# Attention logits of two units at a time, shorter projection stretches, and a written-out order of steps

## The chip, the cores and the metric

The kernel runs on one core of a Trainium2 chip. The metric is the device time of one execution in microseconds (us); smaller is better. Five engines work side by side, each through its own instructions in order: PE (the matrix engine; the trace keeps its weight loads apart as PEld), DVE (vector), ACT (activation), POOL and SP. SP here only starts DMAs. They wait for one another through semaphores.

## The reference

A trunk of two decoder layers over 512 tokens of width 1024, in float32. The first layer (a Mamba-2 mixer and a convolutional feed-forward net) and both feed-forward nets are not touched by this change. The part in question is the differential attention of the second layer, with 8 heads, two softmax maps per head (c = 0, 1) and 64 numbers per map, over keys and values that were projected once:

```python
logits = jnp.einsum('bqhcd,bkhcd->bhcqk', qblk, k).astype(jnp.float32) * scale
logits = logits + bias[None, :, None]
logits = jnp.where(dist >= 0, logits, -jnp.inf)
p = jax.nn.softmax(logits, axis=-1)
attn = p[:, :, 0] - lam * p[:, :, 1]
return jnp.einsum('bhqk,bkhd->bqhd', attn.astype(v.dtype), v)
...
o = rms_norm(o, subln_g) * (1.0 - lam_init)
return o.reshape(b, s, V_TOTAL) @ out_w
```

## The kernel before

Every large product is done as three matmuls of 128x128 weights by 512 columns (high part times high part, high by low, low by high). In the attention stage these large products are the projections: values of heads 0 to 3 (`v0`), queries of heads 4 to 7 (`q1`), values of heads 4 to 7 (`v1`), and the output projection of heads 0 to 3 (`attn_out(0, ...)`). They are chained into one generator, `fill`, and the attention proper is put between pieces of it. A call of `next(fill)` issues the next stretch. In `proj` (L1326) a stretch is two token blocks, which is 12 matmuls; in `attn_out` it is 6.

The attention is cut into units. A head has three: query blocks 0 and 1 together, block 2, and block 3 (`PARTS`), with 384, 384 and 512 columns of keys up to the diagonal. A unit goes through these steps:

- `logits()`: the matmuls at L1514, queries times keys, one bank of PSUM for each of the two maps. The two maps use the two halves of PE's rows and run side by side. Then DVE adds the bias and finds the maximum, from PSUM into SBUF (L1520), and ACT takes the exponential and its sum (L1527).
- `weigh()`: a reciprocal and a small product on DVE (L1532, L1533), then p0 + factor * p1 (L1537).
- `turn()`: 3 or 4 transposes on PE (L1546) into one bank, copied to SBUF by ACT (L1547).
- `values()`: transposed weights times values on PE (L1557) into one bank, copied by ACT (L1560).

When the three units of a head are through, `normed_out` normalises the head on DVE and ACT (L1567 to L1573), and `turned_out` transposes it on PE (L1579), with two copies out (L1583 on ACT, L1584 on DVE).

All these small banks, those of the transposes of keys and queries (L1373, copied by ACT at L1375) too, come from one ring of four auxiliary banks:

```python
def aux_bank(name):
    return pp.tile([P, T], F32, tag="aux", name=name)
```

The fifth request waits until the first bank has been read. The large products have four banks of their own (`mm_bank`). The copies of the values projection out of those banks are at L1480, on ACT; weights are split into high and low parts by ACT (L173, L148) and DVE (L174, L159).

The order on PE in this stage is the order in which the code is written (`manual_schedule` for PE alone); for DVE and ACT a scheduler orders the work, so the lists on those two engines move with the code too. Before the change the order came from a list of "places", from which the code worked out, by counters, which unit is turned, weighed and valued when. Apart from the first place, which does two units' logits together, each place did: transposes of one unit, logits of one unit, weighted values of an earlier unit, then one or two stretches. In the names of the trace, `lg` is logits, `at` transposed weights, `po` weighted values, `oT` the turned head, `ps_v`, `ps_q` and `ps_ao` the banks of the projections; `lg4_2` in an instruction list is head 4, part 2.

Of the kernel before, what the change touches and what calls it, by code (L numbers as in the profile page):

```python
# [42 lines left out]
def trunk_kernel(ctx: ExitStack, tc, x, ssm_ln_g, ssm_in_w, ssm_conv_w, ssm_conv_b, ssm_dt_bias,  # L43
# [60 lines left out]
    def tok_order(key):  # L104
        return (2, 6, 0, 4) if key == "q0" else range(0, KB, 2)
# [1187 lines left out]
    with tc.tile_pool(name="att", bufs=1) as ap, ExitStack() as later:  # L1293
# [32 lines left out]
        def proj(key, evac):  # L1326
            pss = [mm_bank("ps_%s_%d" % (key, b)) for b in range(NT)]
            order = tok_order(key)
            for k0 in order:
                wh, wl = chunk("%s_%d" % (key, k0))  # L1330
                for b in range(NT):
                    ts = slice(b * P, (b + 1) * P)
                    for k in range(k0, k0 + 2):
                        st, sp_ = k == order[0], k == order[-1] + 1
                        pe.matmul(pss[b], xgh[k][:, ts], wh[:, k - k0, :], start=st, stop=False)
                        pe.matmul(pss[b], xgh[k][:, ts], wl[:, k - k0, :], start=False, stop=False)
                        pe.matmul(pss[b], xgl[k][:, ts], wh[:, k - k0, :], start=False, stop=sp_)
# [12 lines left out]

        def squared(key, t, rt, out, b):
            s = ap.tile([P, T], F32, tag="ksq", name="ksq%s_%d" % (key, b), bufs=1)
# [128 lines left out]
            yield from proj(key, evac)  # L1481

        PARTS = ((0, 1), (2,), (3,))
        fl = lambda a: a.rearrange("p a b -> p (a b)")

        class Unit:


            def __init__(self, h, part, st):
                self.h, self.part, self.st = h, part, st  # L1490
                self.tag = "%d_%d" % (h, part)
                self.ii = PARTS[part]
                self.off = (0, P)
# [55 lines left out]
            def values(self):  # L1549
                h = self.h  # L1550
                if self.part == 0:
                    self.st["ot"] = up.tile([P, NT, P], F32, tag="ot", name="ot%d" % h, bufs=2)
                ps = aux_bank("po" + self.tag)
                for j, i in enumerate(self.ii):
                    o = self.off[j]
                    for k in range(i + 1):
                        pe.matmul(ps[:, j * P:(j + 1) * P], self.at[:, o + k * P:o + (k + 1) * P],  # L1557
                                  vt[k][:, h * P:(h + 1) * P], start=(k == 0), stop=(k == i))
                k = len(self.ii)
                act.activation(self.st["ot"][:, self.ii[0]:self.ii[0] + k, :],  # L1560
                               ps[:, :k * P].rearrange("p (a d) -> p a d", a=k), AF.Copy)

        def normed_out(h, st):
            ot = st["ot"]
            sq = ap.tile([P, T], F32, tag="ksq", name="osq%d" % h, bufs=1)
            so = up.tile([P, NT], F32, tag="so", name="so%d" % h, bufs=2)
            act.activation(sq, fl(ot), AF.Square)  # L1567
            dve.reduce_sum(so, sq.rearrange("p (a q) -> p a q", a=NT), axis=AX.X)
            e = up.tile([P, NT], F32, tag="eps", name="eps%d" % h, bufs=2)
            s0 = st["sm"][:, :, 0]  # L1570
            dve.scalar_tensor_tensor(out=e, in0=s0, scalar=EPS, in1=s0, op0=ALU.mult, op1=ALU.mult)
            rsqrt_act(so, ap, "o%d" % h, [P, NT], P, e)
            dve.tensor_tensor(out=ot, in0=ot, in1=so.unsqueeze(2).to_broadcast([P, NT, P]), op=ALU.mult)  # L1573
# [14 lines left out]
        os = []  # L1588
# [45 lines left out]
        with tc.manual_schedule(engines={mybir.EngineType.PE}):  # L1634
            run(qk("q0", qT[0], 49, (("2", 1), ("5", 0))))
            with tc.tile_pool(name="keys", bufs=1) as kc:
                keys(kc)
            op_ = later.enter_context(tc.tile_pool(name="att_o", bufs=1))
            up = later.enter_context(tc.tile_pool(name="units", bufs=1))
            fill = chain(vproj("v0", 0), qk("q1", qT[1], 49, ((2, 0), (2, 1))), vproj("v1", 1),  # L1640
                         attn_out(0, None, range(KB)))
            us = []
            for h in range(AH):
                st = {}
                us += [Unit(h, part, st) for part in range(len(PARTS))]
            n = len(us)

            ots, valued_heads = [], []
            for _ in range(5):
                next(fill)  # L1650

            def values(t):
                u = us[t]
                u.values()
                if u.part == len(PARTS) - 1:
                    valued_heads.append(u)
                    ots.append([t + 5, u])
# [6 lines left out]
            def out_of(t):  # L1664
                if ots and ots[0][0] <= t:
                    u = ots.pop(0)[1]
                    os.append(turned_out(u.h, u.st))

            turned = valued = weighed = t = 0

            def turn_to(m):
                nonlocal turned
                while turned < min(m, n):
                    us[turned].turn()
                    turned += 1

            def weigh_to(m):
                nonlocal weighed
                while weighed < min(m, n):
                    us[weighed].weigh()  # L1680
                    weighed += 1

            def values_to(m):
                nonlocal valued
                while valued < min(m, n):
                    values(valued)
                    valued += 1

            for places in [(2, 2), 1, 1, 1, 1, 1, 1, 1, 1, 2, 1, 1, 1, 1, 1, 2, 1, 2, 1, 2, 1, 2, 2, 1, 1, 1]:
                if isinstance(places, tuple):  # L1690
                    weigh_to(t)
                    turn_to(t - 1)
                    values_to(t - 2)
                    norm_heads()
                    turn_to(t)
                    next(fill)
                    out_of(t + 1)
                    values_to(t)
                    norm_heads()
                    next(fill)  # L1700
                    us[t].logits()
                    us[t + 1].logits()
                    weigh_to(t + 1)
                    next(fill)
                    weigh_to(t + 2)
                    next(fill)
                    t += 2
                    continue
                turn_to(t - 1)
                if t == n - 5:  # L1710
                    weigh_to(t)
                    with tc.issue_after(us[t - 1].weighed):
                        us[t].logits()
                elif t < n:
                    us[t].logits()
                weigh_to(t)
                values_to(t - 2)
                for i in range(places):
                    if places == 1 and t < 16:
                        out_of(t)  # L1720
                    next(fill)
                    if i == 0 and (places > 1 or t > n):
                        out_of(t)
                    if valued_heads and os:
# [3 lines left out]
                t += 1  # L1728
            assert next(fill, None) is None
            last_out(norm1)  # L1730

# [37 lines left out]
```

## Time and profile before

| | |
|---|---|
| median of 3 timed runs | 1318.3 us (1318.17 to 1318.86) |
| the profiled execution | 1318.13 us, of which the span from first to last instruction is 1316.3 us |
| DVE busy over the span | 1069.5 us (81%) |
| ACT busy over the span | 713.6 us (54%) |
| first and last logit matmul of the stage | 811.5 us and 928.8 us from the span's start |
| granted PE clock in this stage | 1.00 |

A matmul that is recorded as busy may overlap the next one, because PE is a pipeline. So the time that a group of matmuls costs is read from one start to the next start, not from the busy column. A matmul with float32 operands (logits and weighted values) appears as two records, two passes with one weight load each; the transposes and the large products appear as one.

### The profile page before, as it was taken

To read this page: it belongs to the slowest core of one execution; us is meant where nothing else is said; L and a number is where in the kernel's file an instruction comes from. 1 tells how busy PE (TensorE), PEld (TensorE's weight loads), DVE (VectorE), ACT (ScalarE), POOL (GpSimd) and SP (SyncE) were. 2 spreads that over 40 slices of the span, in tenths; PEclk is the share of its full clock that TensorE was granted. 3 is DMA by queue.
4 is the path that set the end of the run, shared out by engine and by line. 5 is a ranking of instruction groups with operands and counts; after the bars stand their busy time and mean duration, and the time that the engine had idled before them with its cause. 6 is when DMAs were issued, how large, how long until landed. Compare 5 with 4: busy or idle time off the path is not lost.

```text
span 1316.3 us, 18256 instructions
## 1 busy us (share of the span) xinstructions
PE 1311.2 (100%) x6771; PEld 1096.9 (83%) x6771; DVE 1069.5 (81%) x1774; ACT 713.6 (54%) x1156; POOL 178.1 (14%) x244
## 2 busy tenths in 40 slices
PE   9999999999999999999999999999999999999998
PEld 8878888888888988898889887777788888888887
DVE  7989878888878877876888877677778878887886
ACT  6696554743354445544556667767654544544452
POOL 5230200300021401120113210000020100010001
PEclk9999999999999999999999999999999999999999
DMA  7553433432235657673866754211224445453625
GB/s 209 156 153 90 149 101 108 140 95 85 84 96 138 126 139 204 179 161 113 220 164 145 197 124 128 69 60 64 65 80 160 98 119 183 105 96 112 192 64 128
DMA packets 202552, 167.84 MB, mean 128 GB/s; under 512 B 7580, under 2 KB 175904, under 8 KB 202464
## 3 DMA queue, kind: packets, MB, share of 16 engines
q1 hardware_dynamic: 176080, 124.93, 31.7%
q0 software_dynamic: 22928, 36.46, 14.7%
q10 hardware_dynamic: 3456, 5.30, 1.1%
q8 instruction: 53, 0.87, 0.3%
q14 instruction: 35, 0.29, 0.1%
HBM read 160.21 MB, written 6.44 MB: 127 GB/s over the span
## 4 chain that ended last, share of the span: by engine, by line
PE 98%; ACT 1%; DVE 1%; issue 0%; DVEq 0%
PE ps_g L209 6%; PE ps_u L209 6%; PE ps_g L208 6%; PE ps_u L208 6%; PE ps_u L210 6%; PE ps_g L210 6%; PE ps_in L208 5%; PE ps_in L210 5%; PE ps_in L209 5%; PE ps_s L1239 3%; PE ps_s L1244 3%; PE ps_s L1242 3%; PE ps_s L1144 3%; PE ps_s L1146 3%; PE ps_s L1141 3%; PE ps_o L209 2%
## 5 line engine op out<-in xcount | busy, mean ns | idle before, releaser
L208 PE MATMUL ps_u<-xgh,wh_u 128*128 128x512 f32 x352 | 137.4, 390 | 0.0
L209 PE MATMUL ps_g<-xgl,wh_g 128*128 128x512 f32 x352 | 137.1, 390 | 0.0
L208 PE MATMUL ps_g<-xgh,wh_g 128*128 128x512 f32 x352 | 137.1, 389 | 0.0
L210 PE MATMUL ps_u<-xgh,wl_u 128*128 128x512 f32 x352 | 137.0, 389 | 0.0
L209 PE MATMUL ps_u<-xgl,wh_u 128*128 128x512 f32 x352 | 137.0, 389 | 0.0
L210 PE MATMUL ps_g<-xgh,wl_g 128*128 128x512 f32 x352 | 137.0, 389 | 0.0
L208 PE MATMUL ps_in<-xgh,wh_in 128*128 128x512 f32 x304 | 123.0, 404 | 0.0
L210 PE MATMUL ps_in<-xgh,wl_in 128*128 128x512 f32 x304 | 119.7, 394 | 0.0
L209 PE MATMUL ps_in<-xgl,wh_in 128*128 128x512 f32 x304 | 119.2, 392 | 0.0
L209 PEld LDWEIGHTS ps_g<-xgl,wh_g 128*128 128x128 f32 x352 | 66.1, 188 | 13.8 <-DVE xgl L488 0.3
L210 PEld LDWEIGHTS ps_u<-xgh,wl_u 128*128 128x128 f32 x352 | 66.1, 188 | 13.7
L1244 PE MATMUL ps_s<-sl,wh_s 128*128 128x256 f32 x308 | 77.5, 283 | 0.0
L208 PEld LDWEIGHTS ps_g<-xgh,wh_g 128*128 128x128 f32 x352 | 66.1, 188 | 13.7
L1242 PE MATMUL ps_s<-sh,wh_s 128*128 128x256 f32 x308 | 77.5, 283 | 0.0
L210 PEld LDWEIGHTS ps_g<-xgh,wl_g 128*128 128x128 f32 x352 | 66.1, 188 | 13.6
L208 PEld LDWEIGHTS ps_u<-xgh,wh_u 128*128 128x128 f32 x352 | 66.1, 188 | 13.6
L209 PEld LDWEIGHTS ps_u<-xgl,wh_u 128*128 128x128 f32 x352 | 66.1, 188 | 13.5
L1126 ACT ACTIVATE sh<-vg 128x256 fp32r<-128x256 f32 (+1 forms) x44 | 23.1, 524 | 98.5 <-DVE vg L1276 98.4
L1052 POOL DMA_DIRECT2D wz<-in_ffn_down_w_dram x36 | 44.2, 1296 | 235.8 <-DVE wl_s L1080 167.9
L1024 DVE SCALAR_TENSOR_TENSOR vg<-ug,cf,vg 128x511 f32<-128x511 f32 x88 | 65.8, 747 | 5.5 <-ACT vg L1022 4.1
L1272 ACT ACTIVATE vg<-vg 128x512 f32<-128x512 f32 x44 | 27.8, 633 | 78.2 <-DVE vg L1024 78.1
L1021 DVE TENSOR_TENSOR uu<-ps_u,nr_f 128x512 f32<-128x512 f32 x44 | 30.3, 689 | 46.7 <-PE ps_u L210 46.7
(425 smaller groups left out, 3501.2 us busy)
## 6 DMA issues: line engine op xcount, KB each, us to landing
wr_g<-in_ffn_up_w_dram SPq DMA_DIRECT2D x44, 512.0 KB, 3.9
wr_u<-in_ffn_up_w_dram SPq DMA_DIRECT2D x44, 512.0 KB, 3.9
wr_in<-in_ssm_in_w_dram SPq DMA_DIRECT2D x40, 512.0 KB, 3.8
wz<-in_ffn_down_w_dram POOLq DMA_DIRECT2D x27, 512.0 KB, 5.8
m<-cumd POOLq DMA_DIRECT2D x16, 512.0 KB, 4.7
wr_out<-in_ssm_out_w_dram SPq DMA_DIRECT2D x16, 512.0 KB, 3.4
wr_s<-in_ffn_down_w_dram SPq DMA_DIRECT2D x13, 512.0 KB, 3.7
xT<-in_ffn_down_w_dram SPq DMA_DIRECT2D x10, 512.0 KB, 6.8
```

What stands on the lines that cost most here:

```text
L208: pe.matmul(ps, wh, xh, start=start, stop=False)
L209: pe.matmul(ps, wh, xl, start=False, stop=False)
L210: return pe.matmul(ps, wl, xh, start=False, stop=stop).ins
L1021: dve.tensor_tensor(out=u, in0=ps, in1=r, op=ALU.mult)
L1024: dve.scalar_tensor_tensor(out=v[:, s:], in0=u[:, :T - s], scalar=col(2 - s), in1=v[:, s:], op0=ALU.mult, op1=ALU.add)
L1052: pool.dma_start(view(t, nq), source(p0, c, nq, j, i), accum_op=ALU.add)
L1141: pe.matmul(pss[b], h, ws[q][1][:, cols], start=False, stop=end and q == qs[-1], skip_group_check=more)
L1144: pe.matmul(pss[b], h, ws[q][0][:, cols], start=first and q == qs[0], stop=False, skip_group_check=more)
L1146: pe.matmul(pss[b], w, ws[q][0][:, cols], start=False, stop=False, skip_group_check=more)
L1239: pe.matmul(v[:, b], wl[:, q, cols], h, start=False, stop=q == nq - 1, skip_group_check=not opens or b > 0)
L1242: pe.matmul(v[:, b], wh[:, q, cols], h, start=opens and q + b == 0, stop=False, skip_group_check=not opens or b > 0)
L1244: pe.matmul(v[:, b], wh[:, q, cols], w, start=False, stop=False, skip_group_check=not opens or b > 0)
```

## The change

Three edits. First, `proj` gives way after every token block and not after every second one, so that a stretch of a projection is 6 matmuls. Secondly, the logits of two units are issued together over four auxiliary banks (a step written `L`), followed by the weighing of both. Thirdly, the counters are gone: a string of letters says where each stretch (`f`), each unit's transposes (`a`), each unit's weighted values (`v`) and each turned head (`o`) stands. The amount of computation stays the same: 24 units, 24 turns, 24 values, 64 stretches of 6 matmuls (where it was 24 of 12 and 16 of 6).

```diff
@@ proj
                             for i in (b - 1, b):
                                 evac(i, pss[i], rts[0])
-                        yield
+                    yield
@@
         PARTS = ((0, 1), (2,), (3,))
+        ORDER = ("f f L f f a f",
+                 "L f a f v f v f a f",
+                 "L f a f v f v f a f",
+                 "L f a f v f v f o a f",
+                 "L f a f v f v f o a f",
+                 "L f a f v f v f a f",
+                 "L f a f v f v o a f",
+                 "L f a f v f f v o a f",
+                 "L f a v f v a f",
+                 "L f a v f v o a f",
+                 "L f a v f v o a f",
+                 "L f a v f v a f",
+                 "f a v f o v f")
@@
-            for _ in range(5):
+            for _ in range(10):
                 next(fill)
...
-            for places in [(2, 2), 1, 1, 1, 1, 1, 1, 1, 1, 2, 1, 1, 1, 1, 1, 2, 1, 2, 1, 2, 1, 2, 2, 1, 1, 1]:
...
-                turn_to(t - 1)
-                if t == n - 5:
-                    weigh_to(t)
-                    with tc.issue_after(us[t - 1].weighed):
-                        us[t].logits()
-                elif t < n:
-                    us[t].logits()
-                weigh_to(t)
-                values_to(t - 2)
-                for i in range(places):
-                    if places == 1 and t < 16:
-                        out_of(t)
-                    next(fill)
-                    if i == 0 and (places > 1 or t > n):
-                        out_of(t)
...
+            steps = {"f": lambda: next(fill), "a": lambda: next(turned).turn(), "v": values, "o": head_out}
+            pairs = iter(zip(us[::2], us[1::2]))
+            for step in " ".join(ORDER).split():
+                if step == "L":
+                    pair = next(pairs)
+                    for u in pair:
+                        u.logits()
+                    for u in pair:
+                        u.weigh()
+                else:
+                    steps[step]()
             assert next(fill, None) is None
             last_out(norm1)
```

Two places show what this does to the engines' lists. Lines from L1497 on are 13 higher after the change (L1514 is L1527, L1546 is L1559, and so on).

**The first logits.** On PE, at the boundary between the third and the last weight chunk of `v0`, before (-) and after (+):

```order
 L1336 MATMUL ps_v0_3_7495<-wl_v0_4_7499,xgh_86 128x512
 L1337 MATMUL ps_v0_3_7495<-wh_v0_4_7498,xgl_87 128x512
+L1527 MATMUL lg0_0_0_7622<-kT0_6903,qT0_6905 128x128
+L1527 MATMUL lg0_0_1_7623<-kT0_6903,qT0_6905 128x128
+L1527 MATMUL lg0_0_0_7622<-kT0_6903,qT0_6905 128x256
+L1527 MATMUL lg0_0_1_7623<-kT0_6903,qT0_6905 128x256
+L1527 MATMUL lg0_1_0_7639<-kT0_6903,qT0_6905 128x384
+L1527 MATMUL lg0_1_1_7640<-kT0_6903,qT0_6905 128x384
 L1335 MATMUL ps_v0_0_7492<-wh_v0_6_7530,xgh_86 128x512
 L1336 MATMUL ps_v0_0_7492<-wl_v0_6_7531,xgh_86 128x512
```

The logits of the first two units stand 12 large matmuls earlier than before. On PE, 12 large matmuls further on, where the logits stood:

```order
 L1337 MATMUL ps_v0_1_7493<-wh_v0_6_7530,xgl_87 128x512
-L1514 MATMUL lg0_0_0_7644<-kT0_6903,qT0_6905 128x128
-L1514 MATMUL lg0_0_1_7645<-kT0_6903,qT0_6905 128x128
-L1514 MATMUL lg0_0_0_7644<-kT0_6903,qT0_6905 128x256
-L1514 MATMUL lg0_0_1_7645<-kT0_6903,qT0_6905 128x256
-L1514 MATMUL lg0_1_0_7661<-kT0_6903,qT0_6905 128x384
-L1514 MATMUL lg0_1_1_7662<-kT0_6903,qT0_6905 128x384
+L1559 MATMUL at0_0_7677<-ident_77,lg0_0_0_7620 128x128 x3
 L1335 MATMUL ps_v0_2_7494<-wh_v0_6_7530,xgh_86 128x512
```

Now the first unit's transposes stand there, two stretches behind its logits. On DVE, after the change, between the first reads of these logits and the weighing of the first unit:

```order
L1533 ISA lg0_1_1_7638,mx0_1_7636<-lg0_1_1_7640,tb0_7616 128x384
L1533 ISA mx0_1_7636 128x1
L1545 RECIPROCAL sm0_7618<-sm0_7618 128x2
L174 SCALAR_TENSOR_TENSOR wl_q1_2_7657<-wr_q1_2_7654,c2_89,wh_q1_2_7656 128x512
L1546 SCALAR_TENSOR_TENSOR sm0_7618<-sm0_7618,nlam_94 128x2
L1550 SCALAR_TENSOR_TENSOR lg0_0_0_7620<-lg0_0_1_7621,sm0_7618,lg0_0_0_7620 128x128
L1550 SCALAR_TENSOR_TENSOR lg0_0_0_7620<-lg0_0_1_7621,sm0_7618,lg0_0_0_7620 128x256
```

Before, both halves of the weight split `wl_q1_2` stood ahead of the reads; now one half stands ahead of them and the other inside the weighing.

**The first values of head 4.** They (`po4_0`) are the first to need the second half of the values, which ACT copies from the banks of `v1` into `vt0` to `vt3`. On ACT, before:

```order
L1547 ACTIVATE at4_0_8416<-at4_0_8417 128x384
L1527 ACTIVATE lg4_2_0_8423,sm4_8323<-lg4_2_0_8423,mx4_2_8422 128x512
L1527 ACTIVATE lg4_2_1_8424,sm4_8323<-lg4_2_1_8424,mx4_2_8422 128x512
L1560 ACTIVATE ot3_8344<-po3_2_8436 128x128
L1480 ACTIVATE vt0_6907<-ps_v1_0_8142,tr_nkv_6982 128x512
L1567 ACTIVATE osq3_8462<-ot3_8344 128x512
L1480 ACTIVATE vt1_6908<-ps_v1_1_8143,tr_nkv_6982 128x512
L1547 ACTIVATE at4_1_8477<-at4_1_8478 128x384
```

And on ACT after the change:

```order
L1540 ACTIVATE lg4_2_1_8448,sm4_8332<-lg4_2_1_8448,mx4_2_8446 128x512
L1540 ACTIVATE lg5_0_0_8461,sm5_8459<-lg5_0_0_8461,mx5_0_8460 128x128
L1480 ACTIVATE vt0_6907<-ps_v1_0_8146,tr_nkv_6982 128x512
L1540 ACTIVATE lg5_0_1_8462,sm5_8459<-lg5_0_1_8462,mx5_0_8460 128x128
L1540 ACTIVATE lg5_0_0_8461,sm5_8459<-lg5_0_0_8461,mx5_0_8460 128x256
L1540 ACTIVATE lg5_0_1_8462,sm5_8459<-lg5_0_1_8462,mx5_0_8460 128x256
L1560 ACTIVATE at4_1_8496<-at4_1_8497 128x384
L1480 ACTIVATE vt1_6908<-ps_v1_1_8147,tr_nkv_6982 128x512
L1573 ACTIVATE ot4_8510<-po4_0_8511 128x256
```

The copy `vt1`, without which `po4_0` cannot end, has moved from ahead of the exponentials of `lg5_0` to behind them. On DVE after the change, the reads of the same pair of units, whose results those exponentials need (rows of `mx` alone are the second half of the read above them):

```order
L1533 ISA lg4_2_0_8447,mx4_2_8446<-lg4_2_0_8449,tb4_8330 128x512
L1533 ISA mx4_2_8446 128x1
L501 TENSOR_TENSOR rst_o3_8417<-so3_8411 128x4
L159 TENSOR_TENSOR wl_ao0_1_8487<-wr_ao0_1_8484,wh_ao0_1_8486 128x1024
L502 SCALAR_TENSOR_TENSOR rst_o3_8417<-rst_o3_8417,rsm_o3_8416 128x4
L1533 ISA lg4_2_1_8448,mx4_2_8446<-lg4_2_1_8450,tb4_8330 128x512
L1533 ISA mx4_2_8446 128x1
L503 SCALAR_TENSOR_TENSOR so3_8411<-rst_o3_8417,so3_8411 128x4
L1533 ISA lg5_0_0_8461,mx5_0_8460<-lg5_0_0_8463,tb5_8457 128x128
L1533 ISA mx5_0_8460 128x1
L1586 TENSOR_TENSOR ot3_8306<-ot3_8306,so3_8411 128x512
L1533 ISA lg5_0_1_8462,mx5_0_8460<-lg5_0_1_8464,tb5_8457 128x128
```

Before, the two reads of `lg4_2` stood next to each other; now a weight split (`wl_ao0_1`) stands between them, and a product over a whole head (`ot3`) between the reads of `lg5_0`.

More of the change, by code (lines that the diff above doesn't have):

```diff
@@ L1645, in trunk_kernel @@
                 us += [Unit(h, part, st) for part in range(len(PARTS))]
-            n = len(us)
-            ots, valued_heads = [], []
-            for _ in range(5):
+            for _ in range(10):
                 next(fill)
[L1652 to L1657, printed above, removed]
+            turned, valued = iter(us), iter(us)
+            valued_heads, normed_heads = [], []
             def norm_heads():
@@ L1662, in norm_heads @@
                     normed_out(u.h, u.st)
[L1664 to L1687, printed above, removed]
-            for places in [(2, 2), 1, 1, 1, 1, 1, 1, 1, 1, 2, 1, 1, 1, 1, 1, 2, 1, 2, 1, 2, 1, 2, 2, 1, 1, 1]:
-                if isinstance(places, tuple):
-                    weigh_to(t)
-                    turn_to(t - 1)
-                    values_to(t - 2)
-                    norm_heads()
-                    turn_to(t)
-                    next(fill)
[L1697 to L1700, printed above, removed]
-                    us[t].logits()
[L1702 to L1709, printed above, removed]
-                if t == n - 5:
-                    weigh_to(t)
-                    with tc.issue_after(us[t - 1].weighed):
-                        us[t].logits()
-                elif t < n:
-                    us[t].logits()
-                weigh_to(t)
-                values_to(t - 2)
-                for i in range(places):
-                    if places == 1 and t < 16:
-                        out_of(t)
-                    next(fill)
-                    if i == 0 and (places > 1 or t > n):
-                        out_of(t)
-                    if valued_heads and os:
@@ L1725, in trunk_kernel, with values @@
+                    normed_heads.append(u)
+            def values():
+                u = next(valued)
+                u.values()
+                if u.part == len(PARTS) - 1:
+                    valued_heads.append(u)
+                    if os:
                         with tc.issue_after(state["ol"]):
```

4 lines of the change are left out of this document (3 added, 1 removed).

## The prediction

> **What bounds the kernel now.** I read the page first, then the attention stage alone.
>
> ```profile
> span 1316.3 us, 18256 instructions
> PE 1311.2 (100%) x6771; PEld 1096.9 (83%) x6771; DVE 1069.5 (81%) x1774; ACT 713.6 (54%) x1156; POOL 178.1 (14%) x244
> PE 98%; ACT 1%; DVE 1%; issue 0%; DVEq 0%
> 811.00:942.00 131.00, 130.92 (x737) 99.66 (x736) 96.66 (x307) 93.71 (x250) 0.00 (x0) 1.00 0.21 65
> ```
>
> The chain that ended last is PE for 98% of the span. The last row is the attention stage: of 131.00 us PE is busy 130.92, while DVE and ACT work for 96.66 and 93.71. So PE waits for nobody here, although DVE and ACT are some 70% full. The change can then do two things only: alter what PE's own sequence costs, or make PE wait. Both are read from starts in the timeline.
>
> **What PE's own sequence costs.** The first rows are the one place where two units' logits already stand together; the others show a unit alone, and transposes followed by values with no logits between.
>
> ```profile
> 811.00 0.39 PE L1336 MATMUL ps_v<-wl_v,xgh 128*128 128x512 f32 x1
> 811.23 0.39 PE L1337 MATMUL ps_v<-wh_v,xgl 128*128 128x512 f32 x1
> 811.55 1.57 PE L1514 MATMUL lg<-kT,qT 64*128 64x128 f32 x12
> 813.05 0.50 PE L1335 MATMUL ps_v<-wh_v,xgh 128*128 128x512 f32 x1
> 813.39 0.40 PE L1336 MATMUL ps_v<-wl_v,xgh 128*128 128x512 f32 x1
> ...
> 840.49 0.93 PE L1514 MATMUL lg<-kT,qT 64*128 64x128 f32 x8
> 841.34 0.94 PE L1557 MATMUL po<-vt,at 128*128 128x128 f32 x6
> 842.03 0.48 PE L1335 MATMUL ps_q<-wh_q,xgh 128*128 128x512 f32 x1
> 842.35 0.40 PE L1336 MATMUL ps_q<-wl_q,xgh 128*128 128x512 f32 x1
> 844.86 0.60 PE L1546 MATMUL at<-ident,lg 128*128 128x128 f32 x4
> 845.39 0.92 PE L1514 MATMUL lg<-kT,qT 64*128 64x384 f32 x4
> 846.24 0.94 PE L1557 MATMUL po<-vt,at 128*128 128x128 f32 x6
> ...
> 935.24 0.40 PE L210 MATMUL ps_ao<-oh,wl_ao 128*128 128x512 f32 x1
> 935.48 0.60 PE L1546 MATMUL at<-ident,lg 128*128 128x128 f32 x4
> 935.91 0.83 PE L1557 MATMUL po<-vt,at 128*128 128x128 f32 x6
> 936.50 0.48 PE L208 MATMUL ps_ao<-oh,wh_ao 128*128 128x512 f32 x1
> ```
>
> A large matmul follows the last in 0.23 us (811.00 to 811.23). Four transposes take 0.43 when values come next (935.48 to 935.91), 0.53 when logits come next (844.86 to 845.39): entering the half-row logits costs 0.10. Six records of values take 0.59 after transposes (935.91 to 936.50) and 0.69 after logits (841.34 to 842.03): leaving costs 0.10 in the next group. The two kinds of unit take 0.85 alone (840.49 to 841.34, 845.39 to 846.24), together 1.70, but the pair takes 1.50. Entered from and left for large matmuls, the pair pays the same single tolls (0.32 for 0.23, and 0.34 where 842.03 to 842.35 has 0.32). So a pair saves 0.20 + 0.10 + 0.10 = **0.40 us**. There are 12 pairs afterwards and one before: 11 x 0.40 = **4.4 us saved**. The bounds are 3.9 (the row of 0.34 taken as a full extra toll on that side) and 4.7.
>
> The shorter stretches cut the row of large matmuls oftener. A cut costs nothing I can see: 0.24 from a large matmul to transposes (935.24 to 935.48), and after values 0.32 that makes up for a last record of values shortened by about as much. Some 30 more cuts at 0.00 to 0.01 are under 0.3 us. The multiplications are as many as before. The bias loads of the next head are wanted one unit earlier:
>
> ```profile
> L1500 SPq DMA_DIRECT2D tb<-bd x8: 338/338/425, 792.9 to 903.9; - x8
> DMA to landing us min/median/max: 3.0/3.6/5.2
> ```
>
> They land 3.6 us after issue, and each has two buffers. A unit is 5 us of PE and the second buffer was last read a whole head ago, so I put the SP queue at nothing; if a load came behind a weight load on SP that waits, one L would start up to 3.6 us late.
>
> **Where PE will wait.** Until now, a unit's transposes came two units (10 us) behind its logits. In the new list they come two stretches behind at the start, four or five later, and ACT and DVE must read, exponentiate and weigh two units in that time. I added up the chains in the order that the changed lists have, with these durations.
>
> ```profile
> 812.51 0.29 DVE L1520 CUSTOM_DVE_ANT_0 lg<-lg,tb 128x128 f32<-128x128 f32 x1 [1.40 <-PE lg L1514]
> 812.72 0.42 DVE L1520 CUSTOM_DVE_ANT_0 lg<-lg,tb 128x256 f32<-128x256 f32 x1
> 815.20 0.75 DVE L1537 SCALAR_TENSOR_TENSOR lg<-lg,sm,lg 128x128 f32<-128x128 f32 x2
> 809.70 1.41 DVE L174 SCALAR_TENSOR_TENSOR wl_q<-wr_q,c,wh_q 128x512 fp32r<-128x512 f32 x2 [1.50 <-ACT wh_q L173]
> 850.64 1.13 PE L1514 MATMUL lg<-kT,qT 64*128 64x512 f32 x4
> 851.80 0.69 DVE L1520 CUSTOM_DVE_ANT_0 lg<-lg,tb 128x512 f32<-128x512 f32 x1 [0.70 <-PE lg L1514]
> L159 DVE TENSOR_TENSOR wl_ao<-wr_ao,wh_ao 128x1024 fp32r<-128x1024 f32 x7 | 8.6, 1222 | 2.4 <-ACT wh_ao L148 2.4
> L1573 DVE TENSOR_TENSOR ot<-ot,so 128x512 f32<-128x512 f32 x7 | 4.8, 687 | 0.1
> L1527 ACT ACTIVATE lg<-lg,mx 128x512 f32<-128x512 f32 x16 | 11.5, 717 | 8.5 <-DVE mx L1520 8.5
> L1527 ACT ACTIVATE lg<-lg,mx 128x256 f32<-128x256 f32 x16 | 8.0, 498 | 0.5 <-DVE mx L1520 0.5
> L1527 ACT ACTIVATE lg<-lg,mx 128x128 f32<-128x128 f32 x16 | 6.3, 392 | 2.4 <-DVE mx L1520 2.4
> L1547 ACT ACTIVATE at<-at 128x384 f32<-128x384 f32 x16 | 7.7, 481 | 2.6 <-PE at L1546 2.6
> L1480 ACT ACTIVATE vt<-ps_v,tr_nkv 128x512 f32<-128x512 f32 x7 | 4.6, 675 | 0.7 <-PE ps_v L1337 0.7
> ```
>
> Neighbours overlap: on DVE the next starts 0.08 before the row's end (812.51, 812.72), on ACT about 0.11; an exponential also reads its sum out, so that its step is about its mean.
>
> *First transposes.* Logits move from 811.55 to 808.83 (12 large matmuls). Before, logits to weighed took 815.20 + 0.75 - 811.55 = 4.40 us. Now one half of the weight split (809.70, 0.66) delays the first read from 809.79 to 810.36, and the other half, 0.66, stands inside the weighing, of which the quicker order of exponentials takes back 0.2: weighed at 808.83 + 4.40 + 0.57 + 0.46 = 814.26. PE is there after the pair, 1.50, a toll of 0.11 and two stretches, 12 x 0.23: 813.20. PE waits **1.1 to 1.2**.
>
> *Values of head 4.* Count from the first logit of the pair `lg4_2`, `lg5_0`. PE needs 1.8 (0.4 of pass time more than the pair of 1.50, with its exit), 1.38 for a stretch, 0.33 for three transposes, 1.38 again, and 0.45 for the blocks that need only `vt0`: it wants `vt1` at 5.3. DVE reads `lg4_2_0` at 1.16 (850.64 to 851.80), for 0.61; `wl_ao0_1` takes 1.14 and two tiny steps 0.16; so `lg4_2_1` is read from 3.07 to 3.76. ACT then does its exponential (to 4.5), one of 128 columns (4.9), the copy `vt0` (5.5), exponentials of 0.39, 0.49, 0.49 (6.8), the copy of the transposes, 0.37, and `vt1`, 0.68: 7.9. PE waits **2.6**. Behind it in PE's queue stand the rest of `v1` and all that follows.
>
> *Three in the output projection.* A pair holds all four auxiliary banks, so that the next transposes need DVE's first reads of it. Before `lg6_0`, DVE has two additions and a split `wl_ao0_3`; by the same sums `at5_2` waits 0.6. Its copy on ACT lies behind six exponentials, and `po5_2` waits 0.5; at the next pair `po6_1` waits 0.7 likewise. Ahead of that, `lg1_2` finds its bank still holding turned keys, 0.4.
>
> Together 1.2 + 2.6 + 0.6 + 0.5 + 0.7 + 0.4 = 6.0. A group that starts after a wait also has no weights loaded ahead; by the toll of 0.10 that is about 0.5 for these. Of the present list some 0.2 us of small waits go. So **6.3 us of waits**, with bounds 4.9 (no reload toll, ACT copies 0.2 sooner at each place) and 7.5 (two more places like `at5_2`).
>
> **The sum.** 6.3 - 4.4 = +1.9 us on the profiled execution, 1318.13 to 1320.0; the median of the runs lies 0.17 above that execution, so **1320.2 us**. The bounds give 4.9 - 4.7 = +0.2 to 7.5 - 3.9 = +3.6.
>
> [...]
>
> **Rivals.**
>
> *The waits are smaller than the saving.* The lists of DVE and ACT are fixed, but I took ACT's start behind each wait as late as the sums allow. If ACT and DVE, 70% full, run ahead at head 4, `vt1` is there in time and 2.6 goes; if the bank waits go too, only the start (1.2) and the keys (0.4) stay: 1.6 - 4.4 = -2.8, or 1315.5. Against it stands `wl_ao0_1`, which no order of arrival moves from between the two reads. It decides when `vt1` is copied before 5.3 on that scale.
>
> *The copy of transposed weights always comes last.* Slower: in each of the 11 pairs ACT runs the exponentials of both units ahead of a copy that PE waits for. Six exponentials are 3.0 us, one stretch is 1.38. If PE loses 0.7 in each, beside 1.2, 2.6 and 0.4, that is 7.7 + 4.2 - 4.4 = +7.5, 1325.8; half the pairs give about +3.7, 1322. It decides where a `v` stands one stretch behind an `a` that follows L. For it: in the last four pairs the list has just that. Against it: in the earlier pairs another stretch lies between, and the wait comes out at nothing there.
>
> *The clock falls.* The granted clock is 1.00 in the whole stage. In the kernel's first microseconds 13 records of a 128x128 matmul take 3.14 us, against 0.11 each for values:
>
> ```profile
> 1.14 3.14 PE L292 MATMUL warm<-ones 128*128 128x128 f32 x13 [1.14 <-DVE ones L219]
> ```
>
> So a cold start costs 3.14 - 13 x 0.11 = 1.7 us. If the wait at head 4 cooled PE, the time would be 1321.9. [...]
>
> **How the numbers follow.** The forecast gets 0.60, the smaller waits 0.17, the copies that come last 0.20, the clock 0.03. About 0.2% (2.6 us) is what a measurement here can tell from no change: 1315.7 to 1320.9. Of the forecast's own range, 1318.5 to 1321.9, I put 0.14 above that, of the slower rival 0.13, with the clock 0.30 in all; of the quicker rival 0.15 lies below. The rest, 0.55, is no change that can be told. The range of 8 in 10 goes to the quicker rival's 1315.5 and into the slower one, to 1323.0.
>
> **What would show it.** PE idle, now 0.1 us in the stage, should be about 6 in the profile after, with one wait of over 2 us for `vt` (L1480), one over 1 us for weighed logits at the first transposes, and half-microsecond ones at transposes and values behind the last pairs. A logit pair should take 1.5 to 1.7 us from start to start. Without the wait for `vt` the first rival is right; with waits in every pair the second; with pairs that take as long as two units apart, my saving is wrong.

## The result, and the profile after

| | median | range | runs |
|---|---|---|---|
| before | 1318.18 us | 1317.26 to 1319.03 | 22 |
| changed | 1320.03 us | 1319.09 to 1322.27 | 22 |

The changed kernel takes 1.0016 times the time of the one before (95% interval 1.0009 to 1.0022): 1.85 us more, where 1.9 were forecast. One of the 11 runs of experiment 1 below took 1444.79 us at a mean granted clock of 0.85, and is left out of its ratio. The page of the changed kernel's profile, busy times by engine and then the chain that ended last:

```profile
span 1317.4 us, 18264 instructions
PE 1308.4 (99%) x6771; PEld 1095.3 (83%) x6771; DVE 1071.5 (81%) x1774; ACT 713.3 (54%) x1156; POOL 178.3 (14%) x244
PE 96%; ACT 1%; DVE 1%; DMA 0%; issue 0%; SPq 0%; DVEq 0%; ACTq 0%
```

The attention stage by itself (stretch, its length, then busy time of PE, weight loads, DVE, ACT, POOL, and the granted clock):

```profile
811.00:942.00 131.00, 127.12 (x725) 98.43 (x725) 95.28 (x296) 92.01 (x246) 0.00 (x0) 1.00 0.21 65
```

PE idles 3.88 us of 131.00, where it idled 0.08. What it waited for, from 808 to 943 us (engine, line, what was waited for: us in total, times, longest):

```profile
PE po L1570 <- ACT vt L1480: 2.1, 2, 1.6
PE po L1570 <- ACT at L1560: 0.8, 2, 0.5
PE at L1559 <- DVE lg L1550: 0.6, 1, 0.6
PE at L1559 <- DVE mx L1533: 0.3, 1, 0.3
```

These are four of the five kinds of wait that the prediction named; the one for the bank of turned keys doesn't show as idle time. The prediction's sign of about 6 us of idle time did not come, and its wait of over 2 us for `vt` came as two, of 0.5 and 1.6. The view counts only what lies between the modelled end of one matmul and the start of the next (a large matmul is recorded for 0.39 us where the next starts after 0.23, so some 0.16 of a wait is hidden); the full loss is read from start to start. First how long the stage is: its first large matmul (`ps_v`) and its last (`ps_ao`), each with durations and the first and last start, before:

```profile
L1335 PE MATMUL ps_v<-wh_v,xgh x64: 389/389/504, 790.6 to 894.9; 128*128 128x512 f32 x64
...
L210 PE MATMUL ps_ao<-oh,wl_ao x64: 387/392/400, 898.2 to 963.0; 128*128 128x512 f32 x64
```

and after:

```profile
L1335 PE MATMUL ps_v<-wh_v,xgh x64: 389/397/504, 789.8 to 895.6; 128*128 128x512 f32 x64
...
L210 PE MATMUL ps_ao<-oh,wl_ao x64: 388/389/402, 898.3 to 963.9; 128*128 128x512 f32 x64
```

963.0 - 790.6 = 172.4 before, 963.9 - 789.8 = 174.1 after: the stage is 1.7 us longer. This execution also came 0.8 us earlier to the stage. That is no part of the change: in the 12 traces of this document the stage begins anywhere from 789.6 to 791.0. So its own time, 1319.09, lies only 0.96 above the 1318.13 of the profile before. In medians of 22 runs such differences count for less.

**First transposes.** PE and DVE after the change, in order of time (start, duration):

```profile
811.80 0.17 DVE L1545 RECIPROCAL sm<-sm 128x2 f32<-128x2 f32 x1
811.88 0.73 DVE L174 SCALAR_TENSOR_TENSOR wl_q<-wr_q,c,wh_q 128x512 fp32r<-128x512 f32 x1
812.21 0.39 PE L1337 MATMUL ps_v<-wh_v,xgl 128*128 128x512 f32 x1
812.53 0.21 DVE L1546 SCALAR_TENSOR_TENSOR sm<-sm,nlam 128x2 f32<-128x2 f32 x1
812.78 0.75 DVE L1550 SCALAR_TENSOR_TENSOR lg<-lg,sm,lg 128x128 f32<-128x128 f32 x2
813.19 0.83 PE L1559 MATMUL at<-ident,lg 128*128 128x128 f32 x3 [0.59 <-DVE lg L1550]
813.78 0.47 PE L1335 MATMUL ps_v<-wh_v,xgh 128*128 128x512 f32 x1
```

From the large matmul to the transposes it takes 0.98 us instead of 0.24, and the three transposes take 0.59 instead of 0.25, since the later ones wait for the second weighing: 1.08 lost. The weight split `wl_q` stands inside the weighing for 0.65, from 811.88 to 812.53.

**Values of head 4**, with DVE's and ACT's rows that count:

```profile
887.14 1.22 DVE L159 TENSOR_TENSOR wl_ao<-wr_ao,wh_ao 128x1024 fp32r<-128x1024 f32 x1
888.35 0.69 DVE L1533 CUSTOM_DVE_ANT_0 lg<-lg,tb 128x512 f32<-128x512 f32 x1
890.02 0.40 PE L1337 MATMUL ps_v<-wh_v,xgl 128*128 128x512 f32 x1
890.19 0.67 ACT L1480 ACTIVATE vt<-ps_v,tr_nkv 128x512 f32<-128x512 f32 x1
890.91 0.71 PE L1570 MATMUL po<-vt,at 128*128 128x128 f32 x4 [0.49 <-ACT vt L1480]
892.12 0.47 ACT L1560 ACTIVATE at<-at 128x384 f32<-128x384 f32 x1
892.49 0.67 ACT L1480 ACTIVATE vt<-ps_v,tr_nkv 128x512 f32<-128x512 f32 x1
893.22 0.49 PE L1570 MATMUL po<-vt,at 128*128 128x128 f32 x2 [1.60 <-ACT vt L1480]
893.46 0.48 PE L1335 MATMUL ps_v<-wh_v,xgh 128*128 128x512 f32 x1
```

PE waits twice: until `vt0` is copied (890.02 to 890.91, 0.89 for 0.24) and until `vt1` is (six records from 890.91 to 893.46, 2.55 for 0.59). Together 2.61.

**The smaller ones**, on PE. The first rows are the pair of units that follows the turned keys, with the weight load of its second unit (PEld), which waits for ACT's copy of the keys (`kT`); the next two are the same kind of pair later; then a large matmul and what waits behind it, three times:

```profile
828.05 2.28 PE L1527 MATMUL lg<-kT,qT 64*128 64x384 f32 x8
828.63 0.36 PEld L1527 LDWEIGHTS lg<-kT,qT 64*128 64x128 f32 x2 [0.28 <-ACT kT L1375]
830.27 0.50 PE L1335 MATMUL ps_q<-wh_q,xgh 128*128 128x512 f32 x1
...
862.46 1.77 PE L1527 MATMUL lg<-kT,qT 64*128 64x384 f32 x8
864.16 0.50 PE L1335 MATMUL ps_v<-wh_v,xgh 128*128 128x512 f32 x1
...
910.50 0.39 PE L210 MATMUL ps_ao<-oh,wl_ao 128*128 128x512 f32 x1
911.20 0.66 PE L1559 MATMUL at<-ident,lg 128*128 128x128 f32 x4 [0.32 <-DVE mx L1533]
...
913.52 0.40 PE L210 MATMUL ps_ao<-oh,wl_ao 128*128 128x512 f32 x1
914.23 1.05 PE L1570 MATMUL po<-vt,at 128*128 128x128 f32 x7 [0.31 <-ACT at L1560]
...
922.84 0.40 PE L210 MATMUL ps_ao<-oh,wl_ao 128*128 128x512 f32 x1
923.75 0.94 PE L1570 MATMUL po<-vt,at 128*128 128x128 f32 x6 [0.52 <-ACT at L1560]
```

| term | predicted us | measured us, from these rows |
|---|---|---|
| `at0_0`, first transposes | 1.2 | 1.08 |
| `lg1_2`, bank of turned keys | 0.4 | 2.22 - 1.70 = 0.52 |
| `po4_0`, values of head 4 | 2.6 | 2.61 |
| `at5_2` | 0.6 | 0.70 - 0.24 = 0.46 |
| `po5_2` | 0.5 | 0.71 - 0.24 = 0.47 |
| `po6_1` | 0.7 | 0.91 - 0.24 = 0.67 |
| groups slowed behind a wait | 0.5 | about 0.4 (0.06 to 0.13 each at four places) |
| small waits of the old list that go | -0.2 | about -0.5 |
| pairs and cuts, PE's own sequence | -4.4 | 1.7 - 5.7 = -4.0, by difference |
| **stage** | **+1.9** | **+1.7** |

The last terms come from rows that are not shown. Three of the slowed groups start behind a wait of the table (at 911.20, 914.23 and 923.75); the fourth is a pair of units at 899.31 that takes 1.84 for 1.70. Of the old list's small waits, the logits at 825.27 and 922.84 took 0.24 and 0.15 longer than units of the same kind elsewhere, and two other groups 0.08 each. From start to start the pairs after the change take 1.50 to 1.72, but for these two that wait (2.22 and 1.84).

### The profile page after: what moved, and what is told of

It is laid out like the page before. It is cut to its first block, busy times and chain, and to the rows that moved or that the text cites. A ratio compares the mean times of both kernels' runs of the same rounds, so it can differ in the third digit from the quotient of the medians.

```text
span 1317.4 us, 18264 instructions
## 1 busy us (share of the span) xinstructions
PE 1308.4 (99%) x6771; PEld 1095.3 (83%) x6771; DVE 1071.5 (81%) x1774; ACT 713.3 (54%) x1156; POOL 178.3 (14%) x244
## 4 chain that ended last, share of the span: by engine, by line
PE 96%; ACT 1%; DVE 1%; DMA 0%; issue 0%; SPq 0%; DVEq 0%; ACTq 0%
PE ps_g L209 6%; PE ps_g L210 6%; PE ps_u L210 6%; PE ps_u L209 6%; PE ps_u L208 6%; PE ps_g L208 6%; PE ps_in L208 5%; PE ps_in L210 5%; PE ps_in L209 5%; PE ps_s L1239 3%; PE ps_s L1244 3%; PE ps_s L1242 3%; PE ps_s L1144 3%; PE ps_s L1146 3%; PE ps_s L1141 3%; PE ps_o L209 2%
```

## The experiments

Each was timed beside runs of the kernel before (medians 1317.99 to 1318.15 in the three groups). "The changed kernel" is 1320.03.

**1. The first transposes one stretch later.**

```diff
-        ORDER = ("f f L f f a f",
+        ORDER = ("f f L f f f a",
```

> The first row of the list reads `f f L f f f a`: the first unit's transposes stand one stretch (6 large matmuls, 1.38 us) later, nothing else moves. If PE waits there because the weighing on DVE ends a fixed time after the logits (my theory), the wait of about 1.1 us goes whole and nothing is late in its place: 1.2 us less than the changed kernel, about 1318.8, and the rest of the stage as before. If the wait is made by something that moves along (the projection's own copies on ACT behind the same stretch), it stays near 1 us and the time stays at 1320.0.

Measured: 1319.5 (ratio 1.0011, 1.0002 to 1.002). In its trace the wait at the first transposes is gone and nothing is late there. But the median fell by 0.5, not by 1.2. The profile points to the clock. The granted clock is the third number from the end of these rows; the stretches are cut where the trace's record of the clock changes:

```profile
889.14:892.55 3.41, 1.32 (x9) 0.84 (x7) 2.87 (x12) 3.04 (x11) 0.00 (x0) 1.00 0.57 192
892.55:895.96 3.41, 3.41 (x10) 2.65 (x9) 0.00 (x0) 0.99 (x2) 0.00 (x0) 0.50 0.00 0
895.96:899.37 3.41, 3.41 (x23) 3.05 (x22) 0.60 (x1) 2.35 (x6) 0.00 (x0) 1.00 0.00 0
```

In the stretch with the waits of head 4 PE was busy 1.32 of 3.41 us; for the next 3.41 us it ran at half clock. There the large matmuls follow each other in 0.42 or 0.43 instead of 0.23:

```profile
893.41 0.63 PE L1337 MATMUL ps_v<-wh_v,xgl 128*128 128x512 f32 x1
893.83 0.63 PE L1335 MATMUL ps_v<-wh_v,xgh 128*128 128x512 f32 x1
```

That costs half of 3.41, 1.7 us: more than the edit gave back. So the rival on the clock, which I had at 0.03, does happen in this execution. The runs as a whole show it less neatly: of the other ten, eight have a mean clock of 0.999 and took 1319.26 to 1320.52, and the two with 1.000 took 1319.04 and 1319.37, hardly less. Experiments 4, 9 and 10 bear on it.

**2. The values of head 4 one stretch later.**

```diff
-                 "L f a f v f f v o a f",
+                 "L f a f f v f v o a f",
```

> Row 8 of the list reads `L f a f f v f v o a f`: the values of head 4 stand one stretch (1.38 us) later. If the copy of the values on ACT has a fixed place behind the exponentials of the pair (my theory), the wait of 2.6 us loses just that stretch and 1.2 us of it stay, now all for vt1: 1.4 us less than the changed kernel, about 1318.6. If the copy waits for the stretch itself (its bank ends later when the stretch is later), the wait stays at 2.6 and the time at 1320.0. If the place was only chosen badly, and one stretch is enough to clear the queue, 2.6 us go: 1317.4.

Measured: 1318.42 (ratio 1.0004, 0.9995 to 1.0013), 1.6 less than the changed kernel; 1.26 us of the wait are left in the trace, all for `vt1`. The copy has a fixed place on ACT, as I argued. The slowest of the 11 runs took 1319.6, where the changed kernel reached 1322.27: the long runs are gone too.

**3. The pairs parted.** A stretch stands between the logits of the two units, twelve times.

```diff
                 if step == "L":
                     pair = next(pairs)
+                    pair[0].logits()
+                elif step == "M":
+                    pair[1].logits()
                     for u in pair:
-                        u.logits()
-                    for u in pair:
                         u.weigh()
```

> In each of the 12 places with two units a stretch stands between the first unit's logits and the second's (`L f a` becomes `L f M a`, with M for the second unit's logits and the weighing of both); amount of work and number of stretches stay. My theory has the pair worth 0.40 us through entering, leaving and the change between the passes: undone in 12 places it costs 4.0 to 4.8 us on PE; the waits get shorter by about 2 us (at the first transposes 0.7 for 1.2, at head 4 2.0 for 2.6, the keys 0), so the sum is +2 to +3 us, 1322 to 1323. The rival: logits cost the same wherever they stand and the change is all waits; then shorter waits make it faster than the changed kernel by about 2 us, 1318.

Measured: 1322.42 (ratio 1.0033, 1.0021 to 1.0045). The waits are some 2 us shorter, as expected, and the time is 2.4 longer: what is lost is PE's own sequence. From start to start the stage takes 2.0 more with 2.0 less of waits, so the 12 pairs were worth 4.1 us, 0.34 each. PE at a parted pair:

```profile
839.93 0.40 PE L1337 MATMUL ps_q<-wh_q,xgl 128*128 128x512 f32 x1
840.26 0.93 PE L1527 MATMUL lg<-kT,qT 64*128 64x128 f32 x8
841.12 0.50 PE L1335 MATMUL ps_q<-wh_q,xgh 128*128 128x512 f32 x1
841.45 0.39 PE L1336 MATMUL ps_q<-wl_q,xgh 128*128 128x512 f32 x1
```

Entering 0.33 for 0.23, the unit 0.86, leaving 0.33 for 0.23: the three numbers of the prediction, now for each unit and not for each pair.

**4. `vt1` copied five times**, same data, so that the wait at head 4 grows and nothing else changes.

```diff
-                act.activation(vt[b][:, i * 512:(i + 1) * 512], ps, AF.Copy, scale=rt[:, b:b + 1])
+                [act.activation(vt[b][:, i * 512:(i + 1) * 512], ps, AF.Copy, scale=rt[:, b:b + 1]) for _ in range(5 if (i, b) == (1, 1) else 1)]
```

> ACT copies the second block of the values of heads 4 to 7 (vt1) five times instead of once, same data to the same place: 4 more steps of 0.57 us lie ahead of the first values of head 4. The wait for vt there grows from 2.4 us to about 4.7. If a wait costs only its length, the time rises by 2.3 us to 1322.3 and the granted clock stays at 1.00. If a wait of that length cools PE, the matmuls behind it run slower for a while: by the price of the cold start 1.7 us more, about 1324, with a granted clock under 1.00 behind 895 us. If ACT's copy isn't what PE waits for, nothing changes: 1320.0.

Measured: 1324.78 (ratio 1.005, 1.0037 to 1.0062), 4.75 above the changed kernel, with a mean clock of 0.997 to 0.999 in all five runs. The wait grew by 2.9 in the trace (the five copies take 3.55 us, the one took 0.67), some more than I had put for it; the rest is half clock in the profile, over two steps of 3.41 us, in the first of which PE was still waiting for part of the time. ACT's copy is what PE waits for, and this longer wait cost more than its length: 4.75 us for 2.9.

**5. The short stretches alone**, in the kernel before: every place of 12 large matmuls is given in two halves, with a unit's values between them (`stretch` issues both halves and, between them, what it is given); logits stay single.

```diff
-                        yield
+                    yield
...
-                values_to(t - 2)
                 for i in range(places):
...
-                    next(fill)
+                    stretch(lambda: values_to(t - 2 if i == 0 else 0))
```

> The kernel before with the short stretches alone: its own order, each place of 12 large matmuls given in two halves, and the weighted values of a unit between the halves (some 15 more cuts of the row of large matmuls); logits stay one unit at a time. By the prediction a cut costs 0.00 to 0.01 us: no change, 1318.2 within 0.3. If a change between large and small matmuls has a toll like that of the logits (0.10 each), it is 1.5 us slower: 1319.7.

Measured: 1318.02 beside 1317.99 (ratio 1.0002, 0.9993 to 1.0011). No change; the stage is 0.17 us longer in the trace. There the large matmuls of the stage stand in 47 unbroken rows, before in 34: 13 cuts, so 0.01 a cut.

**6. Two weight splits on POOL.**

```diff
-                self.low()
+                self.low(pool if self.key in ("ao0_1", "ao0_3") else dve)
```

> The changed kernel with two weight splits (wl_ao0_1 and wl_ao0_3, L159) on POOL, which is idle in this stage, instead of DVE; the order of PE stays. If the first reads of the logits on DVE behind these splits are what makes ACT and PE late (my theory), the wait at head 4 goes from 2.6 to about 1.9 and moves to vt0, since the copies keep their place on ACT behind the exponentials; at5_2 and po5_2 (0.5 each) go; at0_0 and po6_1 stay: 1.8 us less, 1318.2. If ACT alone decides (the exponentials' own durations), nothing goes: 1320.0. If POOL's split takes longer than the slack, or slows DVE down, the output projection waits for wl_ao instead and it is slower than 1320.

Measured: 1321.17 (ratio 1.0022, 1.0013 to 1.0031): slower, but not by the third case's mechanism, since no wait for `wl_ao` shows. At `at5_2` and `po5_2` the waits went, 1.1 us with the slowed groups behind them, as my theory has it. At head 4 the wait grew from 2.6 to 3.4, all for `vt0`, and two steps at half clock followed, which cost 2.9 from start to start. These make up the 2.65 by which the stage is longer than in the changed kernel, so without the half clock it would be no longer. POOL and DVE at that place and then at the other split:

```profile
887.60 2.38 POOL L159 TENSOR_TENSOR wl_ao<-wr_ao,wh_ao 128x1024 fp32r<-128x1024 f32 x1 [112.43 <-ACT so L499]
888.12 1.88 DVE L501 TENSOR_TENSOR rst_o<-so 128x4 f32<-128x4 f32 x1
890.12 0.69 DVE L1533 CUSTOM_DVE_ANT_0 lg<-lg,tb 128x512 f32<-128x512 f32 x1
...
913.51 2.40 POOL L159 TENSOR_TENSOR wl_ao<-wr_ao,wh_ao 128x1024 fp32r<-128x1024 f32 x1 [23.53 <-PE lg L1527]
913.95 0.28 DVE L1533 CUSTOM_DVE_ANT_0 lg<-lg,tb 128x128 f32<-128x128 f32 x1
```

The product `rst_o`, 4 columns wide, usually takes 0.16 us. Here it took 1.88 and ended at 890.00, when POOL's split ended (889.98). So DVE's second read came 3.78 us after the first logit (at 886.34), where it came 3.06 after it in the changed kernel (885.29 to 888.35). A later read makes a longer wait: that supports DVE's place in the chain, though from the other side than I meant, and not cleanly, since ACT's list moved as well (`vt0` now stands behind all six exponentials).

**7 and 8. Two other lists without the waits**, o1 and o2, with the pairs kept. o1:

```diff
+        ORDER = ("f f L f f f a",
+                 "L f a f v f v f f a f",
+                 "L a f v f v f a f",
+                 "L f a f v f v f o a f",
+                 "L f a f v f v f o a f",
+                 "L f a f v f v f a f",
+                 "L f a f v f v o f a f",
+                 "L f f f a f v o f a",
+                 "L v a f f v v a a f",
+                 "L f f v o a v a",
+                 "L v v f f a o f",
+                 "L f f a v",
+                 "f v a f a v f o v f")
```

> Another list, with the pairs kept and the same number of each letter: rows `f f L f f f a`, `L f a f v f v f f a f`, `L a f v f v f a f`, `L f a f v f v f o a f` twice, `L f a f v f v f a f`, `L f a f v f v o f a f`, `L f f f a f v o f a`, `L v a f f v v a a f`, `L f f v o a v a`, `L v v f f a o f`, `L f f a v`, `f v a f a v f o v f`. By my sums no wait of over 0.2 us is left in the stage up to the last values, and the pairs' 4 us stay: 1318.2 - 4.2 = 1314.0, with PE idle in the stage for under 0.5 us. If waits belong to the pairs (four banks held at once), they only move and the time stays over 1318.

> The same as the list o1 up to its ninth row, then `L f f v o v a a`, `L v f v f a f`, `L f f a o`, `a v f a f f v f o v v`. By my sums 0.05 us better than o1, which no run can tell: 1314.0. If o1 and o2 differ by over 1 us, a wait that my sums miss decides in the last four pairs.

Measured: 1313.94 (ratio 0.9971, 0.996 to 0.9983) and 1313.67 (0.9969, 0.9957 to 0.998). Both beat both kernels. The stage of o1 from 807 to 943 us, then its first and last large matmuls:

```profile
807.00:943.00 136.00, 135.97 (x778) 107.29 (x777) 101.26 (x315) 96.59 (x256) 0.00 (x0) 1.00 0.21 67
...
L1335 PE MATMUL ps_v<-wh_v,xgh x64: 389/397/504, 789.8 to 890.2; 128*128 128x512 f32 x64
...
L210 PE MATMUL ps_ao<-oh,wl_ao x64: 387/389/400, 891.7 to 958.1; 128*128 128x512 f32 x64
```

PE idles 0.03 us, and the stage takes 168.3 instead of 172.4. So the waits don't belong to the pairs; they belong to the list. Of the 4.1 less, about 0.5 are the small waits of the old list.

**9. Edits 1 and 2 together.**

> The edits of the first two experiments together: the first transposes and the values of head 4 each one stretch later. In the first of them alone the median fell by 0.5 us and not by 1.2, and its profile shows 3.4 us at half clock behind the wait at head 4. If that clock took the rest (my theory now), then with the wait at head 4 cut to 1.2 us the first edit is worth its full 1.1 to 1.2 us: 1317.2, and no execution with a clock under 1.00 in the stage. If the first transposes' wait comes back somewhere else whenever it is removed, it stays at the 0.5 of the first experiment: 1317.9.

Measured: 1317.64 (ratio 0.9996, 0.9987 to 1.0005), between the two figures: 0.8 less than edit 2 alone, with runs that scatter by 0.7 either way. The traces are clearer: the stage takes 1.05 us less than with edit 2 alone, and the mean clock of the profiled run is 1.000 (two of the 11 runs have a mean of 0.999, at 1317.71 and 1317.79, no slower than the rest). So the first transposes' wait goes whole where the clock doesn't interfere.

**10. `vt1` copied three times** (3 for 5 in the edit of experiment 4).

> ACT copies vt1 three times instead of once: the wait for it grows by 1.2 us to about 3.0, behind the 0.5 for vt0. If the clock is halved for one window of 3.41 us behind a window in which PE idles more than half, nearly every execution is halved for at least one: 1320.0 + 1.2 + 1.6 less what the changed kernel's executions already have of it (a third of them), so 1322.3, with a mean clock of 0.999 nearly always. If the fall depends on something else than the length of the wait (the chip's temperature, a moment of its own), a third of the executions have it as before, and the median is 1321.2.

Measured: 1323.6 (ratio 1.0043, 1.0029 to 1.0057), with a mean clock of 0.997 to 0.999 in all five runs. Above either figure, and on the side of the clock: some runs show a mean that takes two halved steps (0.997) where I counted one. Its profile has one, behind a stretch with 0.77 us of work:

```profile
891.81:895.22 3.41, 0.77 (x4) 0.71 (x5) 1.14 (x4) 2.77 (x7) 0.00 (x0) 1.00 0.01 3
895.22:898.63 3.41, 3.41 (x9) 2.64 (x8) 0.00 (x0) 0.82 (x2) 0.00 (x0) 0.50 0.00 0
```

## Why the prediction was right, and where it wasn't

- *PE has nobody to wait for, so the change acts only through PE's sequence and new waits.* Right: the stage is 1.7 us longer in the traces, where the medians are 1.85 apart.
- *A pair saves 0.40.* Shown by parting the pairs: tolls of 0.10 in and out, and 0.86 for a unit alone where two together take 1.50. The sum over the stage gives a little less, 0.34 a pair. The term was 4.4; by difference, with the cuts in it, it is 4.0.
- *A cut costs 0.00 to 0.01.* Right at its upper end: 0.17 for 13 cuts. The prediction's "some 30 more cuts" is miscounted: the trace has 18 (52 rows of large matmuls for 34). They cost some 0.2, about half of what the saving fell short by.
- *Waits of 6.3.* Each wait was there, at its place, and its size is off by at most 0.14; only at head 4 PE waits for `vt0` as well as for `vt1`, where the prediction had put it all on `vt1`. The waits of the change add up to 6.2, where 6.5 were forecast; less the old list's small waits (0.5, not 0.2) that is 5.7 for 6.3.
- *The sum.* Waits 0.6 smaller and a saving 0.4 smaller nearly cancel, so that 1.7 stands beside 1.9. That the medians give 1.85 is partly luck, since they hold some half clock, for which the sum had no term.
- *The SP queue at nothing.* Right: no wait of PE, DVE or ACT for a load (`tb` or weights) appears in the stage.
- *Smaller waits* (the quicker rival): the 2.6 at head 4 did not go by itself. *A copy that always comes last*: only at the places named, not in every pair.
- *The clock.* Here the prediction was wrong, though the time came out close to the forecast. The 0.03 was an estimate: the profile before has the clock at 1.00 in the whole stage, where PE is busy for at least 3.34 us of each step of 3.41, and so it shows nothing of what a wait does to the clock. Experiments 1, 4, 6 and 10 show half clock behind a stretch of 3.41 us in which PE had little work (1.32, 0.30, 0.95 and 0.77 us), even where no single wait was long: in experiment 1 two waits of 0.5 and 1.6 us, the changed kernel's own. In the changed kernel's profile the same waits fell on the border of two stretches:

```profile
888.17:891.59 3.42, 2.93 (x16) 2.01 (x14) 3.35 (x17) 2.51 (x9) 0.00 (x0) 1.00 0.56 187
891.59:895.00 3.41, 1.81 (x10) 1.53 (x10) 1.49 (x5) 1.96 (x7) 0.00 (x0) 1.00 0.12 46
```

  and the clock stayed. Of its 22 runs the five slowest (1321.16 to 1322.27) all have a mean clock of 0.999, which is what one halved step makes of 1319 us (1 - 0.5 x 3.41/1319 = 0.9987); they lie 1.5 to 2.7 above the median of the other 17, 1319.62, where the prediction's price was 1.7. (Two of the 17 show 0.999 as well, and so does one of the 23 runs of the kernel before beside experiments 5 to 8, which took 1318.14 where their median is 1317.99: a mean of 0.999 alone doesn't show a halved step in the stage.) All seven runs with 0.999 have a median of 1321.59, the 15 with 1.000 one of 1319.51. No run of the changed kernel but one has its clock on record step by step, so that those five are halved at head 4 is inferred, not shown; and the means do not order single runs elsewhere (experiment 1; in experiment 4 the one run with 0.999 is the slowest, 1325.01). By these figures an estimate for the clock is 0.4 to 0.5 of the 1.85 us.

## What to carry to other kernels

Where an engine pays a toll on changing from one kind of operation to another, grouping pays, and start-to-start times show by how much (here 0.3 to 0.4 us a pair). But bunched work makes bunched demand on the engines behind it, and the list has to be laid so that each consumer finds its copy ready; with that done, the same pairs gained 4 us where they had cost 2. Work waits out along the instruction lists that the changed program really has, with durations from the old trace. And where the clock follows the load, as PE's did here (0.50 behind stretches of 3.41 us with 0.30 to 1.32 us of work), price a wait by how empty it leaves such a stretch, not by its length alone.

## What the runs showed of the hardware

**The granted clock changed in steps of 3.41 us.** The trace of the kernel before has it on record from 6.42 us after the first instruction, at 1.00, and at 0.50 from 1317.14, behind the last work: 1310.72 us later, 384 steps of 3.413. In the changed kernel's trace the two are at 4.12 and 1318.25, 385 steps apart. In the profiles of experiments 1 and 10 the clock stood at 0.50 for 3.41 us, in those of 4 and 6 for 6.82. Stretches of 3.41 us at full clock in which PE was busy for 1.32 (experiment 1, with 2.1 us of waits), 0.95 (experiment 6), 0.77 (experiment 10) and 0.30 us (experiment 4) were followed by half clock; those with 1.81 (the changed kernel) and 2.03 (experiment 3) were not. So an estimate from these six is that at full clock the border lies between 39% and 53% of the stretch, as the profile counts busy time. A halved step was followed by a second one where PE was busy for only 2.05 (experiment 4) or 2.64 us (experiment 6) of it, and by full clock where it was busy for all 3.41 (experiments 1 and 10). The steps lay differently in these two traces (from 6.42 and from 4.12 us after the first instruction), and the same waits at head 4 left a stretch with 1.32 us of work in experiment 1's profile, with 0.50 behind it, and none with under 1.81 in the changed kernel's, where the clock stayed at 1.00.

**One DVE step ended with POOL's.** In experiment 6 the product `rst_o` on DVE began at 888.12, during POOL's split (887.60 to 889.98), and took 1.88 us, to 890.00; the median of its eight executions in that profile is 0.16. A read of logits on DVE (128 columns) beside the other split (913.51 to 915.91) kept its 0.28. What made the first stand still and not the second, these two rows don't show.
